# A two-layer hybrid trunk: the instruction threads are merged with other durations, and the merged order is what every engine runs

## The chip, the cores and the metric

The kernel runs on one core of a Trainium2 chip. TensorE (PE) multiplies matrices, VectorE (DVE) and ScalarE (ACT) work on rows of 128 partitions, GpSimd (POOL) adds and multiplies in SBUF, and SyncE (SP) issues the transfers. Each engine takes its instructions one after another, in the order in which they stand in its queue, and waits on semaphores for the others. The metric is the device time of one execution in microseconds, the median of several runs.

## The reference, cut to what matters

The input has 512 tokens of 1024 float32 features. It passes two layers of three sub-layers each: a SwiGLU feed-forward (FFN) at half weight, a mixer, another FFN at half weight. Each sub-layer has a norm before and after:

```python
def swiglu(x, w_in, w_out):
    gate, up = jnp.split(x @ w_in, 2, axis=-1)
    return (jax.nn.silu(gate) * up) @ w_out          # 1024 -> 2 x 2816 -> 1024

def macaron_layer(x, mixer, ...):
    x = x + 0.5 * rmsnorm(swiglu(rmsnorm(x, ffn1_pre_g), ...), ffn1_post_g)
    x = x + rmsnorm(mixer(rmsnorm(x, mix_pre_g)), mix_post_g)
    x = x + 0.5 * rmsnorm(swiglu(rmsnorm(x, ffn2_pre_g), ...), ffn2_post_g)
    return x
```

Layer 0's mixer ("mixer 0") runs RWKV-7 on 8 heads of 64 beside a gated linear recurrence (RG-LRU, 512 features), from one input projection into one output projection. Layer 1's mixer ("mixer 1") is stick-breaking attention with 16 heads of 64: sigmoids of the scores and a running product along the keys.

## The kernel before, in words

Features lie on the partitions, tokens along the row. Every large product is made of three matmuls in the rounded type fp32r: each operand is split into a high and a low part, and high*high, high*low and low*high are added up in a PSUM bank (`mm3`). Most are 128x128 by 128x512; near a sub-layer's border they are 256 wide, since the tokens are there taken in two halves (s0, tokens 0 to 255, and s256), so that one half's norm can run while the other half is still being multiplied.

The work is written as threads, Python generators whose steps each note a few instructions (`Queue`): `weights` splits each weight chunk as it lands (ACT casts the high part, DVE subtracts the low part); `main` issues the large products; `unit_ev`, `third_ev` and `out_ev` empty the banks; `finish` and `add` do the post-norm and the residual of a half, `pre`, `low` and `norm` the splitting of the next normed input and its sum of squares. In mixer 0 each pair of heads passes three threads, `pair`, `inverse` and `chain`, each pair's `pair` waiting for the one before; their matmuls are small plain float32 (64x64 and the like). In mixer 1 the thread `group` makes scores, scans and transposes of one group of queries.

What sets the order: `Run` merges the threads. It keeps a clock per engine, asks `cost` what each instruction takes and when others see its result (`gap`), and always emits the instruction that could start first (`key`, ties by the thread's priority). PE work of `main` has the last priority (9). In the kernel before, `MANUAL` is empty: the merge only numbers the instructions (`cur_priority`, shifted a little by `OFFS`), and the tile framework's scheduler then sorts each engine's queue a second time, by its own view of what is ready and by these numbers. In the profile nearly every instruction carries the line of one call, L366 in `emit`; so groups are told apart by their tiles: `wraw` raw weights, `whi`/`wlo` weight parts, `bank` PSUM, `b` everything in SBUF, `par` parameters.

At each border between sub-layers PE runs two kinds of 256-wide matmul with the tile `ones`: `finish` sums the squares of a half of the output (they are added on POOL, tile by tile), and `norm` those of the next input. What follows one of them in PE's queue stands until POOL's additions are there.

Of the kernel before, what the change touches and what calls it, by code (L numbers as in the profile page):

```python
# [13 lines left out]
F32R = mybir.dt.float32r  # L14
# [5 lines left out]
P = 128  # L20
# [14 lines left out]
MANUAL = ()  # L35
# [17 lines left out]
# ---------------------------------------------------------------- host layout  # L53
# [4 lines left out]
def _consts():  # L58
    """Masks of the shapes alone: for mixer 0 and for mixer 1."""
# [102 lines left out]
# ---------------------------------------------------------------- on the chip  # L162
class Arena:
    """SBUF banks, cut into regions of 64-column units. A bank holds float32 or
    float32r (rounded) regions, and changes its kind when it is empty."""
# [13 lines left out]
    def place(self, k, kind, wide=False):  # L179
        """the region that has been free for the longest, empty banks last"""  # L180
# [82 lines left out]
class Ev:  # L263
    """Something that threads wait for"""
# [5 lines left out]
MEM = object()  # L270

# [10 lines left out]
class Queue:  # L282
    """An engine's instructions, noted for the thread that runs"""
# [9 lines left out]
class Run:  # L293
    """Threads of instructions, merged in the order in which they could start by a
    rough clock of the engines. A thread is a generator; what it notes up to a yield
    may start together, and after all of the step before."""

    TABLES = {AF.Silu: (1,), AF.Sigmoid: (2,), AF.Exp: (3,), AF.Sqrt: (4,), AF.Tanh: (2, 3)}
    SLOW = ("tensor_tensor_scan", "scalar_tensor_tensor")
    FAST = ("tensor_copy", "tensor_scalar", "tensor_scalar_mul", "tensor_scalar_add", "tensor_scalar_max", "memset")  # L300

    def __init__(self, nc):
# [10 lines left out]
        self.hot = False  # L313

# [3 lines left out]
    def warm(self, t, c, cols):  # L318
        """the PE's clock: halved after a tick with few columns"""
# [6 lines left out]

    def cost(self, eng, op, a, k, start):
        """microseconds of an instruction, and until another engine sees its result"""
# [4 lines left out]
        if eng == "pe":  # L333
            w, x = a[1], a[2]
            n, rows = size(x), w.shape[0] / P
            if op == "transpose":
                c, cols = max(w.shape[1], 64) / 1000.0, w.shape[1]
            elif w.dtype == F32R:
                c, cols = max(n, 256) / 2400.0, n * rows
            else:  # L340
                c, cols = n / (750.0 if n <= 64 and min(w.shape) <= 64 else 600.0), 2 * n * rows
            return c * self.warm(start, c, cols), 0.25
        if eng == "dve":
            if op == "reciprocal":
                return 0.07 + 6.3e-3 * n, 0.2
# [1677 lines left out]
```

## Time and profile before

| | |
|---|---|
| three runs | 2137.93, 2146.51, 2146.17 us; median 2146.17 |
| profiled execution | span 2139.7 us from the first to the last instruction; its time with what lies around the span is not listed apart |
| PE | busy 2060.2 us (96%), 11916 records; weight loads 1747.1 us (82%) |
| DVE, ACT, POOL | busy 57%, 40%, 23% |
| granted TensorE clock | mean 0.984 of 2.4 GHz |
| stages | FFN 0 to 362, mixer 0 to 714, two FFNs to 1462, mixer 1 to 1744, FFN to the end |

How to read it: PE's busy time is a union of records that overlap, so short waits between small matmuls do not show as idle time; counts per stretch show more. Idle time of the other engines costs nothing by itself.

### The profile page before, as it was taken

What the parts mean: (1) busy time and instruction counts of PE and PEld (TensorE: products, weight loads), DVE (VectorE), ACT (ScalarE), POOL (GpSimd) and SP (SyncE); (2) the same over time, 40 slices, a digit from 0 to 9 for tenths busy, and PEclk for the clock granted to TensorE, in tenths of its full rate; (3) what the DMA queues carried; (4) which work ended last, traced back from release to release, by engine and by line L of the source; (5) the groups of instructions that cost most, each with busy time, mean ns of one, the idle gap of its engine ahead of it and who ended that gap; (6) DMA issues with size and microseconds to landing.
All of it is one profiled execution on the core that took longest, in us unless ns stands there. A gap on an engine that the chain in (4) does not pass through costs nothing. (4 is left out here: it accounts for less than half of the span.)

```text
span 2139.7 us, 29740 instructions
## 1 busy us (share of the span) xinstructions
PE 2060.2 (96%) x11916; PEld 1747.1 (82%) x11916; DVE 1229.3 (57%) x1770; ACT 863.9 (40%) x1370; POOL 488.5 (23%) x480
## 2 busy tenths in 40 slices
PE   8999999899999899999999999999999899999998
PEld 7888889877677887888898888888878789788887
DVE  6344344887786853444466354446899977344443
ACT  6322223555655443222335322233666755322221
POOL 3000013512331620100153010015232354010013
PEclk9999999999999999999999999999999999999999
DMA  5322321322113223223312322231111223333311
GB/s 195 120 93 99 101 96 51 117 58 62 35 52 104 84 82 116 88 99 108 99 60 81 117 92 98 96 99 36 54 56 60 79 80 108 99 98 99 108 51 40
DMA packets 72378, 185.54 MB, mean 87 GB/s; under 512 B 19632, under 2 KB 26928, under 8 KB 72240
## 3 DMA queue, kind: packets, MB, share of 16 engines
q1 hardware_dynamic: 72240, 183.65, 26.7%
q8 instruction: 93, 1.52, 0.3%
q14 instruction: 45, 0.37, 0.1%
HBM read 177.85 MB, written 5.77 MB: 86 GB/s over the span
## 5 line engine op out<-in xcount | busy, mean ns | idle before, releaser
L366 PE MATMUL bank<-b,b 128*128 128x512 f32 (+6 forms) x7350 | 1232.1, 330 | 28.4 <-DVE b L366 19.5
L366 PEld LDWEIGHTS bank<-b,b 128*128 128x128 f32 (+3 forms) x7350 | 1031.6, 181 | 217.8 <-DVE b L366 36.5
L366 PE MATMUL bank<-b,whi 128*128 128x512 f32 (+1 forms) x2460 | 692.4, 365 | 20.5 <-DVE b L366 10.9
L366 POOL TENSOR_TENSOR b<-b,b 128x256 f32<-128x256 f32 (+5 forms) x355 | 364.3, 1039 | 870.7 <-DVE b L366 560.6
L366 DVE TENSOR_TENSOR b<-bank,b 128x512 f32<-128x512 f32 (+7 forms) x441 | 250.6, 582 | 527.7 <-PE bank L366 520.9
L366 PEld LDWEIGHTS bank<-b,whi 128*128 128x128 f32 x2460 | 441.8, 192 | 92.6 <-DVE b L366 14.3
L366 PE MATMUL bank<-b,wlo 128*128 128x512 f32 (+1 forms) x1230 | 447.7, 364 | 0.8 <-DVE wlo L366 0.8
L366 DVE TENSOR_TENSOR b<-wraw,b 128x1024 fp32r<-128x1024 f32 (+1 forms) x194 | 267.9, 1386 | 148.7 <-ACT b L366 130.4
L366 ACT CAST b<-wraw 128x1024 fp32r<-128x1024 f32 (+1 forms) x194 | 196.6, 1024 | 333.7 <-PE bank L366 192.4
L366 PEld LDWEIGHTS bank<-b,wlo 128*128 128x128 f32 x1230 | 235.9, 192 | 34.9 <-issue 1.2
L366 POOL TENSOR_TENSOR b<-b 128x512 f32<-128x512 f32 (+5 forms) x93 | 105.5, 1144 | 683.2 <-DVE b L366 553.3
L366 ACT ACTIVATE b<-b 128x256 f32<-128x256 f32 (+1 forms) x319 | 154.3, 501 | 243.1 <-DVE b L366 204.9
L366 ACT CAST whi<-wraw 128x1024 fp32r<-128x1024 f32 (+2 forms) x143 | 144.9, 1018 | 238.5 <-PE bank L366 170.8
L366 DVE TENSOR_TENSOR wlo<-wraw,whi 128x1024 fp32r<-128x1024 f32 (+2 forms) x143 | 201.3, 1412 | 68.0 <-ACT whi L366 67.4
L366 ACT CAST b<-b 128x512 fp32r<-128x512 f32 (+3 forms) x188 | 104.8, 560 | 220.1 <-POOL b L366 185.6
L366 DVE TENSOR_TENSOR b<-b,b 128x512 fp32r<-128x512 f32 (+12 forms) x234 | 138.2, 599 | 73.5 <-ACT b L366 72.1
L366 DVE SCALAR_TENSOR_TENSOR b<-b,par,b 128x256 fp32r<-128x256 f32 (+5 forms) x209 | 151.8, 780 | 2.5 <-ACT b L366 2.2
L366 DVE TENSOR_TENSOR_SCAN b<-b,b 128x512 f32<-128x512 f32 (+1 forms) x72 | 71.5, 1019 | 7.2 <-ACT b L366 6.8
L366 ACT COPY b<-bank 128x512 f32<-128x512 f32 (+3 forms) x104 | 50.6, 500 | 61.4 <-PE bank L366 54.9
L366 ACT ACTIVATE b<-b,par 128x256 fp32r<-128x256 f32 (+1 forms) x100 | 51.2, 520 | 54.2 <-POOL b L366 47.5
L366 ACT ACT_TABLE_LOAD x49 | 62.9, 1283 | 9.5 <-PE bank L366 8.0
L366 DVE RECIPROCAL b<-b 128x256 f32<-128x256 f32 (+3 forms) x34 | 42.3, 1243 | 22.0 <-ACT b L366 21.9
(52 smaller groups left out, 623.3 us busy)
## 6 DMA issues: line engine op xcount, KB each, us to landing
wraw<-in_w_dram SPq DMA_DIRECT2D x302, 512.0 KB
wraw<-in_w_dram SPq DMA_DIRECT2D x32, 384.0 KB
b<-in_x_dram SPq DMA_DIRECT2D x16, 128.0 KB
l_mix_residual<-b SPq DMA_DIRECT2D x8, 256.0 KB
b<-l_mix_residual SPq DMA_DIRECT2D x8, 256.0 KB
out_dram<-b SPq DMA_DIRECT2D x16, 128.0 KB
rwkv_scores<-b SPq DMA_DIRECT2D x16, 64.0 KB
b<-in_aux_dram SPq DMA_DIRECT2D x2, 256.0 KB
```

Of the source, the lines that this page charges most:

```text
L366: f(*a, **k)
```

## The change

`MANUAL` names all five engines, so the second sorting is off and each queue holds the merge's own order. `cost` is written anew with other durations by operation, shape and place, with a surcharge where DVE and POOL both work in SBUF; `gap` takes the delay to the next engine from a table by both engines. Transfers keep their cost (bytes by 220 GB/s, 2 us to land). `OFFS` has no effect any more, since nothing sorts by it. `CALLS` gives each thread's instructions a source line of their own and does nothing else; comments are gone. The core of the diff:

```diff
-MANUAL = ()
+MANUAL = ("PE", "DVE", "Activation", "Pool", "SP")
...
+    AFTER = {"dve": {"dve": 0.08, "act": 0.11, "pool": 0.2, "pe": 0.135, "sp": 0.15},
+             "act": {"act": 0.1, "dve": 0.135, "pool": 0.18, "pe": 0.155, "sp": 0.15},
...
+    def matmul(self, op, w, x):
+        n = math.prod(x.shape[1:])
+        if op == "transpose":
+            return 0.109 * max(w.shape[1], 64) / P
+        if w.dtype == F32R:
+            return 0.012 + n / 2380.0
...
-                c, cols = max(n, 256) / 2400.0, n * rows
...
-            return c * self.warm(start, c, cols), 0.25
+            return c * (1.0 if self.warm(start, c, cols) < 2 else 1.6), 0.2
...
-            return (0.12 if op in self.SLOW else 0.07) + (0.55e-3 if op in self.FAST else 1.04e-3) * n, 0.2
+            sb = all(x.space != PSUM for x in [a[0], *aps])
+            c = self.vector(op, n, (len(aps), sb))
+            if sb and n >= 64 and self.clock["pool"] > start:
+                c += min(self.clock["pool"] - start, 1.2 * c)
+            self.shared = start + c if sb else 0.0
+            return c, 0.11
...
-        return 0.1 + (1.1e-3 if op in self.FAST else 2.25e-3) * n, 0.15
+        c = {"memset": 0.08 + 0.8e-3 * n, "tensor_scalar": 0.1 + 1.3e-3 * n}.get(op, 0.17 + 2.1e-3 * n)
+        if self.shared > start:
+            c += min(0.3 * c, self.shared - start)
+        return c, 0.1
...
     def gap(self, th, eng):
-        return th.lat if th.eng != eng else {"dve": 0.09, "act": 0.05, "pool": 0.05}.get(eng, 0.0)
+        return self.AFTER[th.eng].get(eng, th.lat) if th.eng else 0.0
...
-        f(*a, **k)
+        CALLS.get(th.gen.__name__, OTHER)(f, a, k)
```

Three places show what moves. In the changed kernel's rows L280 is `weights`, L283 `pre`, L285 `norm`, L274 `unit_ev`, L276 `third_ev`, L287 `add`, L292 `chain` and L309 `main`.

The first is ACT at the start of the program. `CAST ... <-wraw_74` and `<-wraw_75` are the high parts of the fourth and the fifth weight chunk. Before:

```order
L366 CAST b_19_186<-wraw_74 128x1024
L366 ACTIVATE b_7_101<-b_2_92,par 128x256
L366 ACTIVATE b_8_102<-b_3_93,par 128x256 x2
L366 ACTIVATE b_9_103<-b_4_94,par 128x256 x2
L366 ACTIVATE b_5_95<-b_1_91 128x256
L366 CAST b_21_221<-wraw_75 128x1024
```

And now the stretch from the second of the rows behind the fourth chunk's cast to the fifth chunk's cast:

```order
L285 ACT_TABLE_LOAD
L285 ACTIVATE b_19_186<-bank_86,eps 128x256
L283 ACTIVATE b_6_102<-b_1_91,par 128x256
...
L274 ACT_TABLE_LOAD
L274 ACTIVATE b_19_186<-b_19_186 128x256 x2
L283 ACTIVATE b_9_105<-b_4_94,par 128x256
L285 ACTIVATE b_24_304<-b_2_92 128x256
L283 ACTIVATE b_9_105<-b_4_94,par 128x256
L274 CAST b_20_190<-b_19_186 128x256
L280 CAST b_22_258<-wraw_75 128x1024
```

Six instructions stood between the two casts, eighteen stand there now: eight of `pre`, four squares and the root of `norm`, two table loads, three of `unit_ev`.

The second is POOL at the border between the two FFNs. `b_5_95` is the sum of squares; `b_4_94`, `b_3_93` and other tiles written and read in place are the residual (`add`). Before, the last row is the last square of the output's half s256, and the rows ahead of it, up to the `b_61_2695` row, are seven squares of `norm` with two of `third_ev` between them:

```order
L366 TENSOR_TENSOR b_61_2695<-b_61_2695,b_105_7352 128x256
L366 TENSOR_TENSOR b_5_95<-b_5_95,b_105_7352 128x256
L366 TENSOR_TENSOR b_5_95<-b_5_95,b_109_7913 128x256
L366 TENSOR_TENSOR b_5_95<-b_5_95,b_105_7352 128x256 x2
L366 TENSOR_TENSOR b_5_95<-b_5_95,b_99_6226 128x256
L366 TENSOR_TENSOR b_5_95<-b_5_95,b_105_7352 128x256
L366 TENSOR_TENSOR b_5_95<-b_5_95,b_99_6226 128x256
L366 TENSOR_TENSOR b_5_95<-b_5_95,b_101_6255 128x256
L366 TENSOR_TENSOR b_5_95<-b_5_95,b_107_7853 128x256
L366 TENSOR_TENSOR b_5_95<-b_5_95,b_99_6226 128x256
```

Now the last L276 row is that square:

```order
L285 TENSOR_TENSOR b_5_95<-b_5_95,b_108_7908 128x256
L276 TENSOR_TENSOR b_5_95<-b_5_95,b_99_6227 128x256
L287 TENSOR_TENSOR b_71_4086<-b_71_4086,b_107_7907 128x256
L285 TENSOR_TENSOR b_5_95<-b_5_95,b_107_7907 128x256
L287 TENSOR_TENSOR b_4_94<-b_4_94,b_108_7908 128x256 x2
L276 TENSOR_TENSOR b_5_95<-b_5_95,b_108_7908 128x256
L287 TENSOR_TENSOR b_65_3216<-b_65_3216,b_108_7908 128x256
L285 TENSOR_TENSOR b_5_95<-b_5_95,b_101_6257 128x256
L276 TENSOR_TENSOR b_5_95<-b_5_95,b_101_6257 128x256
L285 TENSOR_TENSOR b_5_95<-b_5_95,b_101_6257 128x256
L285 TENSOR_TENSOR b_5_95<-b_5_95,b_99_6227 128x256 x2
L285 TENSOR_TENSOR b_5_95<-b_5_95,b_107_7907 128x256
```

Three squares of `norm` stand ahead of it, and four behind it.

The third is PE near the end of mixer 0, in the fourth `chain`'s last products (64x64). The 512-wide rows are products of `main` for the output projection. Before:

```order
L366 MATMUL bank_88<-b_59_2652,b_66_3320 64x64
L366 MATMUL bank_90<-b_54_2436,whi_79 128x512
L366 MATMUL bank_88<-b_51_2430,b_3_93 64x64
L366 MATMUL bank_88<-b_59_2652,b_66_3320 64x64
L366 MATMUL bank_90<-b_58_2440,whi_79 128x512
L366 MATMUL bank_88<-b_61_2695,b_3_93 64x64
L366 MATMUL bank_90<-b_54_2436,wlo_80 128x512
L366 MATMUL bank_88<-b_59_2652,b_66_3320 64x64
```

Now:

```order
L292 MATMUL bank_89<-b_28_341,b_70_3519 64x64
L292 MATMUL bank_89<-b_3_93,b_52_2374 64x64
L292 MATMUL bank_89<-b_28_341,b_70_3519 64x64
L292 MATMUL bank_89<-b_3_93,b_52_2374 64x64
L292 MATMUL bank_89<-b_71_4086,b_70_3519 64x64
L292 MATMUL bank_89<-b_3_93,b_52_2374 64x64
L292 MATMUL bank_89<-b_71_4086,b_70_3519 64x64
L309 MATMUL bank_85<-b_77_5020,whi_81 128x512
```

Over the whole of the fourth chain, from its first to its last matmul, PE's queue had some 77 products of `main` in between; it has 13 now.

## Rows read from the trace of the kernel before

**Rows 1.** The page: span, and busy time by engine.
```profile
span 2139.7 us, 29740 instructions
PE 2060.2 (96%) x11916; PEld 1747.1 (82%) x11916; DVE 1229.3 (57%) x1770; ACT 863.9 (40%) x1370; POOL 488.5 (23%) x480
```
**Rows 2.** Busy time by stretch: an FFN, mixer 0, mixer 1, an FFN.
```profile
core 0: us, PE busy (x) PEld busy (x) DVE busy (x) ACT busy (x) POOL busy (x), PEclk, DMA share, GB/s
50.00:350.00 300.00, 299.73 (x1350) 249.03 (x1349) 131.83 (x131) 88.20 (x111) 30.02 (x25) 1.00 0.31 102
420.00:698.00 278.00, 269.72 (x2389) 200.84 (x2387) 203.98 (x476) 153.13 (x236) 68.23 (x60) 0.96 0.23 65
1520.00:1718.00 198.00, 181.78 (x1066) 155.86 (x1065) 184.39 (x306) 133.38 (x261) 62.09 (x63) 0.98 0.20 64
1840.00:2100.00 260.00, 260.00 (x1179) 216.69 (x1179) 103.97 (x104) 69.86 (x86) 23.36 (x19) 1.00 0.26 85
```
**Rows 3.** ACT at the start, in order of time: start, us, operation.
```profile
18.86 2.11 ACT L366 ACTIVATE b<-b,par 128x256 fp32r<-128x256 f32 x5
21.18 1.04 ACT L366 CAST b<-wraw 128x1024 fp32r<-128x1024 f32 x1
22.11 0.72 ACT L366 ACTIVATE b<-b 128x256 f32<-128x256 f32 x2
26.67 1.28 ACT L366 ACT_TABLE_LOAD   x1
27.97 0.47 ACT L366 ACTIVATE b<-bank,eps 128x256 f32<-128x256 f32 x1
30.26 0.42 ACT L366 ACTIVATE b<-b 128x256 f32<-128x256 f32 x1 [0.58 <-DVE b L366]
```
**Rows 4.** PE at the start, in order of time.
```profile
23.36 5.98 PE L366 MATMUL bank<-b,b 128*128 128x256 f32 x47
38.14 0.70 PE L366 MATMUL bank<-b,ones 128*128 128x256 f32 x2 [1.48 <-POOL b L366]
```
**Rows 5.** PE and POOL at the border between the two FFNs, in order of time.
```profile
1107.78 4.23 PE L366 MATMUL bank<-b,b 128*128 128x256 f32 x34
1115.99 1.22 PE L366 MATMUL bank<-b,ones 128*128 128x256 f32 x2 [3.99 <-POOL b L366]
...
1093.45 8.85 POOL L366 TENSOR_TENSOR b<-b,b 128x256 f32<-128x256 f32 x10 [2.08 <-DVE b L366]
1104.55 11.39 POOL L366 TENSOR_TENSOR b<-b,b 128x256 f32<-128x256 f32 x9 [0.58 <-ACT b L366]
```
**Rows 6.** Matmuls of mixer 0 (420 to 698) by shape, count, busy us and mean ns.
```profile
L366 PE MATMUL bank<-b,whi 128*128 128x512 f32 x303 | 109.4, 424 | 1.6 <-DVE b L366 1.6
L366 PE MATMUL bank<-b,wlo 128*128 128x512 f32 x152 | 64.5, 425 | 0.0
L366 PE MATMUL bank<-b,b 128*128 128x512 f32 x51 | 17.0, 422 | 0.4 <-DVE b L366 0.4
L366 PE MATMUL bank<-b,b 64*64 64x64 f32 x928 | 44.0, 230 | 1.0 <-DVE b L366 1.0
```
**Rows 7.** PE in the middle of mixer 0, in order of time.
```profile
538.87 4.44 PE L366 MATMUL bank<-b,b 64*128 64x512 f32 x89
543.25 0.66 PE L366 MATMUL bank<-par,b 128*128 128x128 f32 x4
546.34 1.11 PE L366 MATMUL bank<-par,b 128*128 128x128 f32 x4 [2.44 <-POOL b L366]
```
**Rows 8.** PE at the end of mixer 0, in order of time.
```profile
698.41 1.22 PE L366 MATMUL bank<-b,whi 128*128 128x512 f32 x4 [0.63 <-ACT b L366]
713.60 1.22 PE L366 MATMUL bank<-b,ones 128*128 128x256 f32 x2 [4.21 <-POOL b L366]
```
**Rows 9.** DVE's form of `low` and of the post-norm: ns min/median/max.
```profile
L366 DVE SCALAR_TENSOR_TENSOR b<-b,par,b x209: 379/946/1831, 6.2 to 2121.3; 128x256 fp32r<-128x256 f32 x48, 128x256 f32<-128x256 f32 x44, 128x511 f32<-128x511 f32 x7, 128x510 f32<-128x510 f32 x2
```
**Rows 10.** Busy time and clock around a wait of PE at the border to mixer 0.
```profile
395.00:405.00 10.00, 6.63 (x41) 6.25 (x41) 9.78 (x15) 6.21 (x17) 5.37 (x9) 0.83 0.51 191
405.00:415.00 10.00, 10.00 (x84) 9.95 (x83) 5.61 (x13) 3.13 (x7) 5.62 (x7) 1.00 0.08 28
```

More of the change, by code (lines that the diff above doesn't have):

```diff
@@ L270 @@
 MEM = object()
+CALLS = {
+    "unit": lambda f, a, k: f(*a, **k),
+    "unit_ev": lambda f, a, k: f(*a, **k),
+    "third": lambda f, a, k: f(*a, **k),
+    "third_ev": lambda f, a, k: f(*a, **k),
+    "out_ev": lambda f, a, k: f(*a, **k),
+    "proj": lambda f, a, k: f(*a, **k),
+    "out_sum": lambda f, a, k: f(*a, **k),
+    "weights": lambda f, a, k: f(*a, **k),
+    "loads": lambda f, a, k: f(*a, **k),
+    "presplit": lambda f, a, k: f(*a, **k),
+    "pre": lambda f, a, k: f(*a, **k),
+    "low": lambda f, a, k: f(*a, **k),
+    "norm": lambda f, a, k: f(*a, **k),
+    "post": lambda f, a, k: f(*a, **k),
+    "add": lambda f, a, k: f(*a, **k),
+    "last": lambda f, a, k: f(*a, **k),
+    "one": lambda f, a, k: f(*a, **k),
+    "pair": lambda f, a, k: f(*a, **k),
+    "inverse": lambda f, a, k: f(*a, **k),
+    "chain": lambda f, a, k: f(*a, **k),
+    "rglru": lambda f, a, k: f(*a, **k),
+    "gelu": lambda f, a, k: f(*a, **k),
+    "result": lambda f, a, k: f(*a, **k),
+    "gate": lambda f, a, k: f(*a, **k),
+    "lora": lambda f, a, k: f(*a, **k),
+    "begin": lambda f, a, k: f(*a, **k),
+    "scores": lambda f, a, k: f(*a, **k),
+    "head": lambda f, a, k: f(*a, **k),
+    "attend": lambda f, a, k: f(*a, **k),
+    "group": lambda f, a, k: f(*a, **k),
+    "unit_v": lambda f, a, k: f(*a, **k),
+    "v_ev": lambda f, a, k: f(*a, **k),
+    "out": lambda f, a, k: f(*a, **k),
+    "home": lambda f, a, k: f(*a, **k),
+    "stash": lambda f, a, k: f(*a, **k),
+    "unstash": lambda f, a, k: f(*a, **k),
+    "main": lambda f, a, k: f(*a, **k),
+    "finish": lambda f, a, k: f(*a, **k),
+}
+OTHER = lambda f, a, k: f(*a, **k)
 class Thread:
@@ L313, in __init__ @@
         self.hot = False
+        self.shared = 0.0
     TICK = 3.413
@@ L325, in warm, with vector @@
         return 1.0 if self.hot else 2.0
+    def matmul(self, op, w, x):
[4 more added lines that the diff above has]
+            return 0.012 + n / 2380.0
+        rows, cols = w.shape[0], math.prod(w.shape[1:])
+        if n <= 2:
+            return 0.112
+        if rows <= 64 and cols <= 64:
+            return 0.045 * n / 64
+        if n <= 64:
+            return 0.054 if cols <= 64 else 0.08
+        return 0.02 + 4 * n / 2380.0 * (0.5 if cols <= 64 or rows <= 64 else 1.0)
+    def vector(self, op, n, ins):
+        full, sb = ins
+        if op == "reciprocal":
+            return 0.06 + 6.3e-3 * n
+        if op == "tensor_tensor_scan":
+            return 0.06 + 2.1e-3 * n
+        if full == 1 and sb and op != "tensor_reduce":
+            return 0.06 + 0.65e-3 * n
+        return 0.065 + 1.04e-3 * n
     def cost(self, eng, op, a, k, start):
```

22 lines of the change are left out of this document (10 added, 12 removed).

## The prediction

> **What bounds the kernel now.** I read the page's busy line first [rows 1]: of 2139.7 us PE is busy 2060.2, so all idle time that PE shows is 79.5 us, 3.7% of the span; DVE has 57%, ACT 40%, POOL 23%. Then the busy times by stretch [rows 2]. In an FFN (50 to 350 us) PE is busy 299.73 of 300 us, DVE 132, ACT 88, POOL 30: nothing but PE counts there, and 1350 matmuls at .222 us each stay whatever their order. The change moves instructions and neither adds nor removes arithmetic, so about 1,400 of the 2140 us, the FFNs, can't change inside. What can change is the start, the borders between stages, and the two mixers, where the small steps of `chain`, `unit`, `third` and `inverse` pass from engine to engine. In mixer 1 (1520 to 1718) DVE, at 184.39 of 198 us, is fuller than PE at 181.78 [rows 2].
>
> The median of the three runs, 2146.17, is 6.5 us above the profiled span. I work out a new span and add 6.5.
>
> **The start.** PE's first long row begins at 23.36 [rows 4], when the fifth weight chunk's high part has been cast: ACT's cast row for that chunk starts at 21.18 and takes 1.04, so it ends at 22.22; the five `pre` activations ahead of it took 2.11, .42 each [rows 3]. In the new order eighteen instructions stand between the fourth chunk's cast and the fifth's, where six stood. Priced by the rows of the same operations: eight `pre` 8 × .42 = 3.4; four squares 4 × .36 = 1.4 (.72 for two); two table loads 2 × 1.28 = 2.6; the root .47; two activations of `unit_ev` at .42, .8; one 256-wide cast, taken as one activation, .4. That is 9.1 us. The stretch begins behind the fourth chunk's cast, which before was over about 18.0, just ahead of the five `pre`; 18.0 + 9.1 + 1.04 = 28.1, against 23.36 when PE now begins with that chunk. So PE waits some 5 us. What could hide it is PE's work on the first four chunks, which is used up by then; were all of it spread by other products that now stand earlier, the cost is 0, and with waits of ACT for POOL and DVE among these eighteen it is 8. I take +5, range 0 to +8. Why the merge does this: it still prices a transfer at bytes by 220 GB/s plus 2 us, so the clock at which it believes the chunk arrives is not this trace's.
>
> **The borders.** Between the two FFNs PE stops 3.99 us for POOL [rows 5]. The last square of the output's half s256 is on POOL, behind seven squares of `norm`; ten such operations take 8.85 us, .885 each. Now three squares stand ahead of it: 4 × .885 = 3.5 us earlier at best. But four `add`s, all of which `norm` of s0 needs, now stand among them, and on PE the ones-matmul that waits for the s256 sum comes 28 products earlier than before: rows 5 give 34 such products 4.23 us, .124 each, so 3.5 us of cover is gone from ahead of the wait. Gain and loss cancel. The next product in the queue is `norm`'s, whose four `add`s (4 × .885 = 3.5 us) are late next. At the border to mixer 0 the same pattern gave a wait of about three microseconds and then a stretch at granted clock .83 on average [rows 10], that is, part of it at 1.2 instead of 2.4 GHz; a border wait costs itself and up to about as much again. I see one wait shortened and others lengthened there (the ones-matmuls of `norm` stand earlier on PE too; at 38.14 one already waits 1.48 us for POOL [rows 4]). Four borders, each ±2.5: 0, range −10 to +10.
>
> **Mixer 0** (420 to 698). PE shows only 278 − 269.72 = 8.3 us idle [rows 2], which would be the least that waits hold. But the records of small matmuls overlap, so I also count. 303 + 152 + 51 = 506 products are 512 wide [rows 6]; at .222, as in the FFN, they are 112 us. The other 2389 − 506 = 1883 records, at .050 (89 of the 64-wide triangle's in 4.44 us [rows 7]), are 94 us. Sum 206, so waits hold at most 278 − 206 = 72 us. A third reading lies between: weight loads are busy 200.84 of 278, 72%, against 249.03 of 300, 83%, in the FFN; at the FFN's density the same loads would take 200.84 / .83 = 242 us, so 36 us are waits. Where those come from can be seen singly: at 543.9 PE stops 2.44 us for POOL before four small products [rows 7] whose operand is a transposed tile of the first chain, and eight ready products of `inverse` stood behind them; the new order has eleven other instructions in between. An order made with durations near the trace's can fill such waits because DVE (73%), ACT (55%) and POOL (25%) have room. Between 8.3 and 72 I go by the nearest stretch, the 36, and take 6 off for the end of the mixer, which comes apart below: −30, range 0 to −72.
>
> The page "Perfetto Trace Analysis" of the Trainium skill, section "Identifying the Most-Contended Engine", says that busy matmul time is a poor measure since matmuls are pipelined, and that weight-load time is a good one. By the busy share alone (97%) the mixer could give back 8.3 us and the sum would be about zero; by the weight loads' (72%), 36. The counts of rows 6 agree with the page.
>
> **The end of mixer 0.** Over the fourth chain some 77 products of `main` stood between its matmuls and 13 do now. 64 × .222 = 14.2 us of cover is moved behind or ahead of it. If the chain runs at the pace of its latencies, the mixer gets longer by all of that; if the products fill what was empty before, by nothing. Behind the mixer PE stopped 4.21 us for POOL, until 713.60 [rows 8], and the products moved back can stand there: 14.2 − 4.2 = 10. I take +10, range 0 to +14.2.
>
> **Mixer 1.** DVE is idle 198 − 184.39 = 13.6 us and PE 16.2 [rows 2]. With DVE at 93% no order gains more than about 13; I take half, −7, and since DVE could also be delayed by POOL (62 us busy beside it), the range is +5 to −13.
>
> The remaining edits are priced at nothing: `CALLS` only labels lines; `OFFS` only served the second sort; SP's queue holds no work that PE waits for behind the start, DMA engines being 20 to 31% busy by stretch [rows 2]; at the start they are in the term above.
>
> **Sum.** +5 + 0 − 30 + 10 − 7 = −22. Span 2139.7 − 22 = 2117.7, and with 6.5 the time is 2124.
>
> **Rivals.**
>
> B, no change: the waits are not misfits of the order but latencies from engine to engine, and durations that no table of constants can give. For it: DVE's one form of `low` and the post-norm takes 379 to 1831 ns, median 946 [rows 9], for much the same tiles; a fixed queue order made with one price is wrong by up to a microsecond at each step, whichever price. And a sort that had placed instructions by its own times of arrival is taken away. Against it: waits such as that at 543.9 are plain misplacements. Then the mixers give back some 5 us, which the start takes: 2146.
>
> The page "SBUF — State Buffer" of the Trainium skill, section "Who interferes with whom", says that DVE and GpSimd hold their shared SBUF ports exclusively, for a whole instruction, so that the second one blocks until the first is done. The new cost is a smooth surcharge, at most 1.2 of DVE's duration; under a lock, who waits is decided by which comes first, and an order computed ahead of time would miss it. The spread of rows 9, 379 to 1831, agrees with the page more than with a surcharge; by that rule the mixer term would be near 0.
>
> C, slower: the fourth chain of mixer 0 loses its fill. With 13 products instead of 77 beside it PE runs on the chain's latencies from about 660 us, the 14.2 us of products follow later as work in addition, and the sparse stretch risks the lower clock as in rows 10. With the start's 5, and mixers that give nothing back, 2146 + 14.2 + 5 = 2165. It decides as soon as what the rest of both mixers gives back is less than about 8 us: 19 − 8 = 11, half a per cent over. For it: PE is bound by work almost everywhere, so cover given away early is missing later. Against it: products used earlier in the mixer are used where PE waited, so they are not lost.
>
> That the change does not do what it says is in part already so: transfers aren't priced from the trace, which is the start's term.
>
> **How the numbers follow.** Half a per cent, about what a measurement of this kernel can tell, is 10.7 us: 2135.4 to 2156.9 is the same. My forecast, 2124, with its own range of 2100 to 2140, has .55, of which .05 lies within the half per cent; B .22, near 2146; C .23, around 2165. Faster .50, same .27, slower .23. The bounds of all terms together (−95 to +37) are wider than I believe at once, since mixer 0 can't give back every latency; below I stop at 2096 (mixer 0 at −58), above at 2166, just past C's price.
>
> **What would show it.** Start: the fifth chunk's cast ends near 28, and PE has a wait of 5 us there. Border between the FFNs: POOL's wait stays 3 to 5 us. Mixer 0: its length falls from 278 towards 250 with the weight loads' share rising from 72% towards 80%, and the 2.44 us wait at 543.9 is gone; in its fourth chain waits for DVE and ACT show on PE, and the 4.21 at its end is gone. Mixer 1: DVE above 95%. I am wrong if the weight loads' share in mixer 0 stays at 72% (B), or if the stretch from the fourth chain's start to the next FFN's first product is longer by more than 14 us (C).

## The result and the profile after

The changed kernel takes 2152.41 us, median of ten runs (2148.02 to 2158.26); the kernel before, in the ten runs beside them, 2141.75 (2137.67 to 2146.51). The ratio is 1.0054, with a 95% interval of 1.0039 to 1.0069: slower by about 11 us, where 22 us less were forecast.

First the page of the changed kernel, span and busy time, which answers to [rows 1]:

```profile
span 2150.2 us, 29766 instructions
PE 2048.2 (95%) x11916; PEld 1751.8 (81%) x11916; DVE 1211.3 (56%) x1770; ACT 858.1 (40%) x1369; POOL 501.9 (23%) x480
```

The work is the same, the span 10.5 us longer. Where, the busy times by stretch tell (columns as in [rows 2]; mixer 0 and mixer 1 lie a little later now):

```profile
50.00:350.00 300.00, 299.73 (x1343) 248.41 (x1342) 128.76 (x132) 87.57 (x111) 32.71 (x21) 1.00 0.32 104
427.00:725.00 298.00, 270.55 (x2566) 218.41 (x2565) 226.52 (x505) 164.34 (x257) 80.76 (x79) 0.94 0.25 73
1532.00:1728.00 196.00, 182.54 (x1060) 158.10 (x1059) 179.40 (x300) 133.93 (x258) 62.57 (x64) 0.97 0.22 70
1840.00:2100.00 260.00, 259.20 (x1143) 214.08 (x1142) 106.75 (x107) 73.34 (x90) 28.06 (x17) 1.00 0.29 92
```

And mixer 0 of the kernel before, between the same two products of `main`:

```profile
415.00:724.00 309.00, 296.10 (x2566) 225.53 (x2565) 228.44 (x509) 168.62 (x260) 83.94 (x74) 0.96 0.23 67
```

The FFNs stand still, as [rows 2] let expect. Mixer 0 is 11 us shorter, with the same 2566 matmuls. So some 22 us must have been lost elsewhere. To find them I counted the products of `main` in PE's order, which is the same list in every kernel, and took the times at which certain ones begin. A stretch "FFN to mixer 0" runs from the last product of the FFN to the 235th of the mixer (behind a mixer or between FFNs to the 469th; into mixer 1 to the 290th). The rest of each FFN differs by at most 0.4 us between any two kernels. The first row of the table is the kernel before in us; all others are differences to it. It holds all experiments, since most of them are read from it. Each row comes from one execution; ten executions of the kernel before lie up to 9 us apart (2137.67 to 2146.51), so a few microseconds in one cell can be what a single kernel does by itself.

| kernel | start | FFN to mixer 0 | mixer 0 | to FFN | FFN to FFN | FFN to mixer 1 | mixer 1 | to FFN | five borders |
|---|---|---|---|---|---|---|---|---|---|
| before | 42.1 | 37.4 | 308.9 | 91.8 | 85.3 | 46.7 | 230.1 | 85.5 | 346.7 |
| changed | +6.7 | +5.0 | -11.6 | -4.1 | +7.0 | +4.6 | -2.7 | +5.9 | +18.5 |
| new_costs_sorted | -1.2 | +1.4 | +18.9 | -1.1 | +4.6 | +5.4 | +1.9 | +2.3 | +12.7 |
| old_costs_unsorted | +7.0 | +12.3 | -2.0 | +0.4 | +8.8 | +8.5 | +1.7 | +10.0 | +40.0 |
| sorted_no_offsets | +3.8 | +7.9 | -24.9 | +2.3 | +4.6 | +3.4 | 0.0 | +6.9 | +25.1 |
| new_sorted_no_offsets | +4.0 | +9.3 | -19.8 | -3.5 | +5.3 | +1.6 | +4.9 | +7.4 | +20.2 |
| no_chain_offset | -0.4 | -1.1 | -17.5 | +0.2 | 0.0 | 0.0 | +0.1 | +0.6 | -0.3 |
| start_faster_loads | +3.4 | +9.1 | -9.0 | -4.0 | +2.9 | +3.6 | -0.4 | +7.4 | +19.0 |
| norm_after_low | +6.6 | +3.6 | -10.0 | -1.0 | +4.9 | -0.5 | -2.8 | +4.7 | +11.7 |
| norm_in_turn | +7.2 | +3.5 | -3.7 | -4.7 | +4.1 | +1.4 | -3.8 | +8.7 | +12.9 |
| norm_in_turn_start | +1.0 | +0.4 | -6.0 | -5.3 | +4.4 | +1.5 | -3.7 | +8.7 | +9.6 |
| norm_both_in_turn | +1.5 | -0.3 | -2.1 | -6.5 | +1.4 | -0.9 | -1.2 | +5.2 | -1.0 |
| nudge_delay | +6.1 | +6.1 | -0.7 | -4.4 | +3.1 | +4.7 | -4.4 | +5.9 | +15.4 |
| nudge_delay_2 | +7.1 | +4.9 | -11.6 | -3.5 | +4.8 | +3.8 | +1.3 | +6.5 | +16.6 |
| nudge_before | -0.6 | +1.0 | +9.8 | -3.9 | -0.7 | +3.8 | +9.7 | +3.8 | +4.0 |
| nudge_before_2 | -0.8 | -0.4 | +26.2 | -3.9 | +0.7 | +2.9 | +4.1 | +5.6 | +4.8 |

The changed kernel loses 6.7 us at the start and 18.5 at the borders, and its mixers give back 14.3.

**The start.** ACT of the changed kernel, answering to [rows 3]; the first row is the fourth chunk's cast, the last the fifth's:

```profile
16.43 1.03 ACT L280 CAST b<-wraw 128x1024 fp32r<-128x1024 f32 x1
...
17.89 1.28 ACT L285 ACT_TABLE_LOAD   x1
...
23.58 1.28 ACT L274 ACT_TABLE_LOAD   x1
...
26.90 1.04 ACT L280 CAST b<-wraw 128x1024 fp32r<-128x1024 f32 x1
```

PE, answering to [rows 4]:

```profile
21.18 3.04 PE L309 MATMUL bank<-b,b 128*128 128x256 f32 x24
27.99 0.80 PE L309 MATMUL bank<-b,b 128*128 128x256 f32 x2 [3.78 <-ACT b L280]
30.59 5.15 PE L309 MATMUL bank<-b,b 128*128 128x256 f32 x29 [1.80 <-DVE b L280]
```

The cast ended at 27.94 where 28.1 had been worked out, and PE waited for it (3.78), and then for the low part of the same chunk (1.80). From 28 to 32 us the granted clock was .50.

**A border.** DVE of the changed kernel between the two FFNs. L310 is `finish` (root and post-norm of the second half), L274 `unit_ev` of the first half:

```profile
1113.44 1.75 DVE L285 RECIPROCAL b<-b 128x256 f32<-128x256 f32 x1
1115.11 0.39 DVE L310 SCALAR_TENSOR_TENSOR b<-b,par,b 128x256 f32<-128x256 f32 x1
1115.41 0.42 DVE L274 TENSOR_TENSOR b<-bank,b 128x256 f32<-128x256 f32 x1
1116.21 0.42 DVE L274 TENSOR_TENSOR b<-bank,b 128x256 f32<-128x256 f32 x1 [0.38 <-PE bank L309]
1119.08 0.42 DVE L274 TENSOR_TENSOR b<-bank,b 128x256 f32<-128x256 f32 x1 [2.44 <-PE bank L309]
1119.42 3.52 DVE L310 SCALAR_TENSOR_TENSOR b<-b,par,b 128x256 f32<-128x256 f32 x5
```

Behind the first of eight post-norm operations stand three `unit_ev` of the other half, and the third waits 2.44 us for a product; seven post-norms stand behind it, which need nothing that the first one did not have. POOL, which adds what they give (L287), answers with a wait:

```profile
1115.58 0.73 POOL L287 TENSOR_TENSOR b<-b,b 128x256 f32<-128x256 f32 x1 [3.96 <-DVE b L310]
1119.97 0.91 POOL L287 TENSOR_TENSOR b<-b,b 128x256 f32<-128x256 f32 x1 [3.66 <-DVE b L310]
1120.85 0.92 POOL L274 TENSOR_TENSOR b<-b 128x256 f32<-128x256 f32 x1
1121.73 1.80 POOL L287 TENSOR_TENSOR b<-b,b 128x256 f32<-128x256 f32 x2
1123.50 0.92 POOL L274 TENSOR_TENSOR b<-b,b 128x256 f32<-128x256 f32 x1
...
1130.53 0.91 POOL L287 TENSOR_TENSOR b<-b,b 128x256 f32<-128x256 f32 x1
```

In the kernel before the same eight adds are one row:

```profile
1120.11 7.09 POOL L366 TENSOR_TENSOR b<-b,b 128x256 f32<-128x256 f32 x8 [4.17 <-DVE b L366]
```

7.09 us there, 15.9 (1115.58 to 1131.44) in the changed kernel. The first half's eight adds, which lie ahead of these rows, are stretched too, by squares of `third_ev` (L276) and of `norm` (L285) among them. Their first and their last:

```profile
1090.08 0.91 POOL L287 TENSOR_TENSOR b<-b,b 128x256 f32<-128x256 f32 x1 [2.26 <-DVE b L310]
...
1103.09 0.91 POOL L287 TENSOR_TENSOR b<-b,b 128x256 f32<-128x256 f32 x1
```

That is 13.9 us; the kernel before has the same eight, with two squares between them, in the 8.85 us of [rows 5]. PE waits for `low` (L284) of either half, which comes behind that half's adds. Its rows, answering to [rows 5]; the first three wait for the first half's `low`, the last three for the second half's:

```profile
1102.59 0.62 PE L309 MATMUL bank<-b,b 128*128 128x256 f32 x3 [0.92 <-DVE b L284]
1103.46 0.62 PE L309 MATMUL bank<-b,b 128*128 128x256 f32 x3 [0.25 <-DVE b L284]
1106.00 4.25 PE L309 MATMUL bank<-b,b 128*128 128x256 f32 x16 [1.92 <-DVE b L284]
...
1130.90 0.62 PE L309 MATMUL bank<-b,b 128*128 128x256 f32 x3 [0.26 <-DVE b L284]
1131.77 0.62 PE L309 MATMUL bank<-b,b 128*128 128x256 f32 x3 [0.25 <-DVE b L284]
1133.51 6.18 PE L309 MATMUL bank<-b,b 128*128 128x256 f32 x39 [1.12 <-DVE b L284]
```

None of these waits is as long as the single 3.99 us of [rows 5], and their sum is not much more (4.7 us in the rows shown). What differs is the clock. Busy times in 5 us of the changed kernel:

```profile
1106.00:1111.00 5.00, 5.00 (x18) 4.07 (x18) 5.00 (x4) 2.91 (x6) 4.76 (x5) 0.50 0.46 142
1111.00:1116.00 5.00, 4.43 (x19) 4.15 (x19) 4.18 (x5) 2.37 (x4) 1.04 (x2) 0.51 0.49 173
...
1131.00:1136.00 5.00, 3.63 (x17) 3.22 (x18) 3.00 (x5) 2.04 (x4) 2.06 (x3) 0.69 0.00 0
```

and of the kernel before, its only stretch below 1.00 there:

```profile
1115.00:1120.00 5.00, 4.00 (x19) 3.83 (x20) 2.56 (x4) 0.47 (x1) 0.94 (x1) 0.66 0.47 156
```

PE shows 5.00 of 5.00 us busy and does 18 matmuls where the full clock does 42 ([rows 10]: 84 in ten). It was fed operand by operand, and the granted clock was 1.2 GHz for ten microseconds, then low once more. An estimate of what the clock took, from PE's busy time in these stretches: 5.00 × .50 + 4.43 × .49 + 3.63 × .31 = 5.8 us, against 4.00 × .34 = 1.4 before, so 4.4 of the 7.0 us that this border lost. By halves: after 48 of the border's products the changed kernel is 9.2 us behind; the kernel before loses 6.2 of this in its own wait of 3.99 us and the slow stretch after it (2.9 are left at the 144th product); the second half's waits add 5.1 by the 216th.

At the border to mixer 1 the second half alone does it. `unit_ev` and what follows it stand on DVE ahead of six of the second half's eight `low`, and PE waits, first in the changed kernel, then in the kernel before:

```profile
1505.84 0.58 PE L309 MATMUL bank<-b,whi 128*128 128x256 f32 x1 [7.61 <-DVE b L284]
1494.34 0.39 PE L366 MATMUL bank<-b,whi 128*128 128x256 f32 x1 [3.03 <-DVE b L366]
```

### The profile page after: what moved, and what is told of

It reads as the page before. It is cut to its first block, busy times and chain, and to the rows that moved or that the text cites. A ratio compares the mean times of both kernels' runs of the same rounds, so it can differ in the third digit from the quotient of the medians.

```text
span 2150.2 us, 29766 instructions
## 1 busy us (share of the span) xinstructions
PE 2048.2 (95%) x11916; PEld 1751.8 (81%) x11916; DVE 1211.3 (56%) x1770; ACT 858.1 (40%) x1369; POOL 501.9 (23%) x480
## 5 line engine op out<-in xcount | busy, mean ns | idle before, releaser
L309 PE MATMUL bank<-b,b 128*128 128x512 f32 (+1 forms) x5379 | 1060.3, 355 | 31.8 <-DVE b L284 25.0
L309 PEld LDWEIGHTS bank<-b,b 128*128 128x128 f32 x5379 | 896.7, 192 | 176.5 <-DVE b L284 32.5
L309 PE MATMUL bank<-b,whi 128*128 128x512 f32 (+1 forms) x2488 | 700.6, 366 | 22.7 <-DVE b L284 9.8
L309 PEld LDWEIGHTS bank<-b,whi 128*128 128x128 f32 x2488 | 451.8, 193 | 96.1 <-DVE b L284 11.6
L309 PE MATMUL bank<-b,wlo 128*128 128x512 f32 (+1 forms) x1244 | 452.7, 364 | 0.5 <-DVE b L291 0.5
L274 DVE TENSOR_TENSOR b<-bank,b 128x512 f32<-128x512 f32 (+1 forms) x237 | 145.3, 619 | 403.4 <-PE bank L309 402.7
L280 DVE TENSOR_TENSOR b<-wraw,b 128x1024 fp32r<-128x1024 f32 (+1 forms) x192 | 255.3, 1330 | 94.0 <-ACT b L280 93.9
L280 ACT CAST b<-wraw 128x1024 fp32r<-128x1024 f32 (+1 forms) x192 | 195.6, 1023 | 211.3 <-PE bank L309 153.6
L309 PEld LDWEIGHTS bank<-b,wlo 128*128 128x128 f32 x1244 | 240.9, 194 | 34.6 <-DVE wlo L280 1.4
L280 ACT CAST whi<-wraw 128x1024 fp32r<-128x1024 f32 (+2 forms) x145 | 147.2, 1017 | 252.5 <-PE bank L309 170.6
L280 DVE TENSOR_TENSOR wlo<-wraw,whi 128x1024 fp32r<-128x1024 f32 (+2 forms) x145 | 198.8, 1372 | 52.6 <-ACT whi L280 52.5
L274 POOL TENSOR_TENSOR b<-b 128x512 f32<-128x512 f32 (+1 forms) x50 | 71.7, 1437 | 571.9 <-DVE b L274 538.0
L274 ACT CAST b<-b 128x512 fp32r<-128x512 f32 (+3 forms) x160 | 88.7, 555 | 278.3 <-POOL b L274 269.1
L274 POOL TENSOR_TENSOR b<-b,b 128x512 f32<-128x512 f32 (+1 forms) x50 | 74.7, 1496 | 503.1 <-DVE b L274 464.9
L276 DVE TENSOR_TENSOR b<-bank,b 128x256 f32<-128x256 f32 (+1 forms) x88 | 47.9, 544 | 191.8 <-PE bank L309 191.6
L274 DVE TENSOR_TENSOR b<-b,b 128x512 fp32r<-128x512 f32 (+3 forms) x140 | 90.1, 646 | 74.2 <-ACT b L274 73.4
L274 ACT ACTIVATE b<-b 128x512 f32<-128x512 f32 (+1 forms) x100 | 57.3, 577 | 107.8 <-DVE b L274 107.8
L287 POOL TENSOR_TENSOR b<-b,b 128x256 f32<-128x256 f32 x87 | 81.2, 944 | 25.9 <-DVE b L310 25.9
L285 POOL TENSOR_TENSOR b<-b,b 128x256 f32<-128x256 f32 x84 | 78.3, 932 | 35.7 <-ACT b L285 34.3
L284 DVE SCALAR_TENSOR_TENSOR b<-b,par,b 128x256 fp32r<-128x256 f32 x96 | 70.5, 766 | 2.3 <-ACT b L283 2.2
L276 POOL TENSOR_TENSOR b<-b,b 128x256 f32<-128x256 f32 (+1 forms) x51 | 43.7, 856 | 98.1 <-ACT b L276 98.1
```

The source lines that it names most:

```text
L274: "unit_ev": lambda f, a, k: f(*a, **k),
L276: "third_ev": lambda f, a, k: f(*a, **k),
L280: "weights": lambda f, a, k: f(*a, **k),
L284: "low": lambda f, a, k: f(*a, **k),
L285: "norm": lambda f, a, k: f(*a, **k),
L287: "add": lambda f, a, k: f(*a, **k),
```

## The experiments

**The two halves of the change apart.** The change has two parts, the second sorting off and the new durations, and four combinations.

new_costs_sorted, the changed kernel with

```diff
-MANUAL = ("PE", "DVE", "Activation", "Pool", "SP")
+MANUAL = ()
```

> The changed kernel with the second sorting switched on again (MANUAL empty), so only the new durations differ from the kernel before. Theory 1 (the lost second sorting makes the start and the borders longer, the new durations make the mixers shorter): the start and four borders come back to the kernel before's lengths, mixers stay 12 and 6 us shorter, so about 2125 to 2132 us, a ratio of 0.991 to 0.996 to the kernel before. Theory 2 (the new durations themselves order the borders badly): still about 2150, ratio 1.003 to 1.006. Theory 3 (the sorting undoes what the merge does, whatever its durations): 2142, ratio 0.998 to 1.002.

2172.01 us, ratio 1.0152 (1.0134 to 1.0169). The start comes back (-1.2), the borders only from 18.5 to 12.7, and mixer 0 is 18.9 us longer. Between the FFNs DVE has the kernel before's order again (below), and the loss has another place: the ones-matmul of [rows 5] waits 8.41 us instead of 3.99, since a square of `third_ev` stands on POOL behind those of `norm`:

```profile
1134.47 1.22 PE L310 MATMUL bank<-b,ones 128*128 128x256 f32 x2 [8.41 <-POOL b L276]
```

old_costs_unsorted, the kernel before with the reverse of that line.

> The kernel before with the second sorting off on all five engines and its old durations kept: the other half of the change. Theory 1: start and borders get longer by 20 to 30 us and nothing is given back in the mixers, so 2162 to 2185 us, ratio 1.010 to 1.020. Theory 2: within 0.3% of the kernel before, 2142 us. Theory 3: the same as theory 1, since a merge by rough durations needs the sorting.

2187.71 us, ratio 1.0220 (1.0204 to 1.0236). By the ratios the sorting off alone costs 47 us, the durations alone 33, both together 12: they are not to be added. Without sorting the new durations give 35 us back (2188 to 2152), 21 of them at the borders; under the sorting they cost 33, 19 of them in mixer 0. No theory had the first run right; theory 1 comes near in the second and has the place of the loss: start and borders lose 25 us in the one kernel without sorting and 47 in the other, where it named 20 to 30. Theory 2 has a part: with the new durations the borders lose 12.7 us even under the sorting.

**What the sorting did at the borders.** It held `norm`, `weights` and `unit_ev` back by 100, 50 and 50 places (`OFFS`). DVE's order between the two FFNs, with L and l for the `low` of the first and second half, N for the root of the first half, u for its `unit_ev` out of the banks; what else stands between them is left out:

```
before               L L L L L L L L l l l l l l l l N u u u u u u
changed              L L L L L L L L N u u u u u l l l u l l l l l
sorted_no_offsets    L L L L L L L L N u u u u u l l l u l l l l l
new_costs_sorted     L L L L L L L L l l l l l l l l N u u u u u u
```

sorted_no_offsets, the kernel before with

```diff
-OFFS = {"norm": -100, "weights": -50, "unit_ev": -50, "chain": -20}
+OFFS = {}
```

> The kernel before with an empty table OFFS: the second sorting stays, but norm, weights, unit_ev and chain are no longer held back in it by 100, 50, 50 and 20 places. If the holding back of norm and unit_ev at the borders is what the changed kernel lost: the borders get longer by 10 to 25 us, 2152 to 2167 us, ratio 1.005 to 1.012. If it is the sorting by times of arrival as such: within 0.2% of the kernel before.

2146.31 us, ratio 1.0028 (1.0016 to 1.0039). The borders lose 25.1 us and the start 3.8, with the old durations and the sorting: so much the holding back was worth there, and the changed kernel has lost it. With the new durations it is worth less: the borders lose 12.7 us with it (new_costs_sorted) and 20.2 without it (new_sorted_no_offsets, below). So the changed kernel's 18.5 us are not all the lost table; the new durations order the borders worse by themselves. What was not expected is that mixer 0 gets 24.9 us shorter, and so the time is below the 2152 to 2167 us expected. `chain` was the likeliest entry for that.

no_chain_offset, the same with only `"chain": -20` taken out.

> The kernel before with chain taken from OFFS (norm, weights and unit_ev stay held back in the second sorting). With an empty OFFS the borders cost 29 us more and mixer 0 gave 25 back. If the holding back of chain by 20 places is what costs mixer 0 those 25 us: borders as in the kernel before, mixer 0 about 284 us instead of 309, 2113 to 2122 us, ratio 0.987 to 0.993. If mixer 0 gained from the other entries of OFFS: within 0.3% of the kernel before, 2134 to 2146 us.

2124.69 us, ratio 0.9929 (0.9909 to 0.9948): the borders as before (-0.3), mixer 0 shorter by 17.5. This is the fastest kernel of the study, faster than both, if 3 us above the expected range: mixer 0 is 291 us long and not 284. Holding `chain` back costs mixer 0 some 20 us: with it and the sorting mixer 0 was 309, 319, 328 and 335 us long in four kernels, without it 284, 289 and 291.

new_sorted_no_offsets, the changed kernel with the sorting on and `OFFS` empty.

> The changed kernel with the second sorting on and OFFS empty. With OFFS the new durations under the sorting gave 2172 us, with 19 us lost in mixer 0 against the kernel before and the borders nearly as before. If what costs mixer 0 there is the holding back of chain, unit_ev and weights: mixer 0 gives back 25 to 45 us, the borders lose 20 to 30, 2145 to 2175 us, and mixer 0 is 270 to 285 us long. If the sorting's own times of arrival spoil the order in mixer 0: it stays at 320 us or more, and the time is 2190 to 2200.

2151.04 us, ratio 1.0048 (1.0032 to 1.0064). Mixer 0 falls from 327.7 to 289.1: the sorting does not spoil the new durations there, the holding back did. That it was `chain`'s is shown with the old durations alone.

**The start.** start_faster_loads, the changed kernel with

```diff
-            return max(0.5, a[0].shape[0] * size(a[0]) * 4 / 220e3), 2.0
+            return max(0.5, a[0].shape[0] * size(a[0]) * 4 / (350e3 if start < 40 else 220e3)), 2.0
```

> The changed kernel, with transfers that the merge places before 40 us of its clock priced at 350 GB/s (the trace shows 330 to 380 in full slices) instead of 220; all else as in the changed kernel. If the start's loss of 7 us comes from the place of the fifth chunk's cast behind eighteen instructions: the cast ends 3 to 5 us earlier, the wait of 3.8 and 1.8 us on PE at 24 us is gone, and the time is 2145 to 2149, ratio to the kernel before 1.002 to 1.004. If another wait takes its place: 2152, ratio 1.005.

2155.84 us, ratio 1.0076 (1.0061 to 1.0091). The start got 3.3 us shorter as expected (the fifth chunk's cast at 22.94 instead of 26.90, one wait of 1.48 left), but the border behind it 4.1 us longer and mixer 0 2.6: one price at the start moves ties in the whole program. The total was a miss, the start a hit.

**The borders mended in the merge.** norm_after_low, the changed kernel with one line of `norm`:

```diff
-            yield Ev(self.run.new.t + LAG[2])
+            yield Ev(self.run.new.t + LAG[2]) if sub.first else self.h_ev[sub, HALVES[1].start, KT - 1]
```

> The changed kernel with one line of norm altered: from the second sub-layer on, the root of the first half (its ones-matmuls, reciprocal and so the unit_ev behind it) waits in the merge for the last low of the second half, which is the order that the kernel before has at all five borders and the changed kernel at none. If the borders' 18 us in the changed kernel come from that (the adds, pre and low of the second half stand among unit_ev and norm of the first): DVE's stretch from the reciprocal of finish to the last low falls from 20 to about 11 us, each border gets 3 to 6 us shorter, 2130 to 2140 us, ratio to the kernel before 0.996 to 1.001. If it is the durations and delays in general: 2148 to 2156, ratio 1.004 to 1.008.

2145.79 us, ratio 1.0017 (1.0004 to 1.0031). That lies between the two ranges expected. DVE's order is as before, the borders lose 11.7 instead of 18.5. Between the FFNs the rest is a wait that the edit itself made; PE there:

```profile
1127.18 0.59 PE L285 MATMUL bank<-b,ones 128*128 128x256 f32 x2
1132.02 1.22 PE L285 MATMUL bank<-b,ones 128*128 128x256 f32 x2 [4.25 <-POOL b L285]
```

The second half's ones-matmul stood right behind the first half's, and its squares still among the adds on POOL.

norm_in_turn keeps this wait for the first half's root alone and puts the squares of the second half behind its last add:

```diff
+            if s.start and not sub.first:
+                yield self.x_ev[sub, s.start, KT - 1]
             for k in range(KT):
...
-            yield Ev(self.run.new.t + LAG[2])
+            yield Ev(self.run.new.t + LAG[2]) if sub.first or s.start else self.h_ev[sub, HALVES[1].start, KT - 1]
```

> The changed kernel with two lines in norm, from the second sub-layer on: the first half's root waits for the last low of the second half (as in norm_after_low), and the second half's squares wait for the second half's last add. In norm_after_low the squares still stood between POOL's adds (10.8 to 12.4 us for eight instead of 7.1), and the second half's ones-matmul stood right behind the first half's on PE, which waited 4.25 us there. If interruption of the second half's chain is what the borders lose: eight adds take 7.1 us again, the wait of 4.25 is gone, the five borders come within 5 us of the kernel before's in sum, 2128 to 2138 us, ratio 0.994 to 0.999. If not: the borders still lose 12 us or more, 2142 to 2152.

2158.15 us, ratio 1.0085 (1.0070 to 1.0099): a miss. The eight adds took 7.1 us again, but the wait did not go, it moved to the same ones-matmul at its new place:

```profile
1140.28 1.16 PE L285 MATMUL bank<-b,ones 128*128 128x256 f32 x2 [4.21 <-POOL b L285]
```

The borders lost 12.9, so an uninterrupted chain alone isn't it: what stands behind the wait in PE's queue counts too.

norm_in_turn_start adds the price of start_faster_loads, and the same order of halves in the first sub-layer.

> norm_in_turn, with the root of the first sub-layer's first half behind the second half's last low too, and transfers before 40 us priced at 350 GB/s in the merge. If the start's 6.5 us are the fifth chunk's cast and the same interruption: product 234 of the first FFN is issued at 42 to 44 us instead of 48.8, and the time is 4 to 7 us below norm_in_turn. If the start is bound by something else: 47 us or later, no difference.

2143.71 us, ratio 1.0016 (1.0006 to 1.0026). The start is at +1.0 instead of +7.2: there the price and the order together were the cause. The time fell by 14 us where 4 to 7 were expected; 6 of them are the start.

norm_both_in_turn takes the two waits that were left: the squares of the first half behind its last add too, and 4 us in `LAG[2]` for the second half's ones-matmul.

```diff
-            if s.start and not sub.first:
+            if not sub.first:
                 yield self.x_ev[sub, s.start, KT - 1]
...
+            yield Ev(self.run.new.t + (0.0 if sub.first or not s.start else LAG[2]))
```

> norm_in_turn_start, with two more edits from the second sub-layer on: the first half's squares wait for the first half's last add as well (they stood among the adds on POOL, and low of the first half ended 4 us later than in the kernel before), and the second half's ones-matmul is placed as if its sum of squares came 4 us later (PE waited 4.5 us at it between the FFNs, with products ready behind it). If these two waits, with the half clock behind each, are what the borders still lose: the border between the two FFNs and that to the last FFN fall to at most 2 us above the kernel before's, all four borders to -8 to +2 in sum, and the time is 2126 to 2138 us, ratio 0.993 to 0.999, mixer 0 anywhere between 297 and 308. If other waits take their place: 2140 to 2150.

2135.28 us, ratio 0.9981 (0.9970 to 0.9993). Time, mixer 0 and the sum of the borders (-1.0) are within what was expected. POOL's adds of the second half between the FFNs:

```profile
1112.70 7.08 POOL L287 TENSOR_TENSOR b<-b,b 128x256 f32<-128x256 f32 x8 [1.34 <-DVE b L310]
```

So what the changed kernel lost at start and borders, 25 us, is undone by three rules in `norm`, a delay and one price, with its durations and without the sorting. The sum is even, but not each border: that behind mixer 0 is 6.5 us shorter than in the kernel before, and that to the last FFN stays at +5.2 where at most 2 were expected. Nor did the first half's part go: between the FFNs this kernel is 7.2 us behind after 48 products, since PE still waits for the first half's `low` there. And mixer 0, at -2.1, gives less than in the changed kernel.

**How far the order alone moves the time.** nudge_delay changes one delay in `AFTER`:

```diff
-             "pe": {"pe": 0.0, "dve": 0.2, "act": 0.2, "pool": 0.25, "sp": 0.25},
+             "pe": {"pe": 0.0, "dve": 0.21, "act": 0.2, "pool": 0.25, "sp": 0.25},
```

> The changed kernel with the delay from PE to DVE in the table AFTER at 0.21 instead of 0.20 us, which says nothing new about the chip. It measures how far the time moves when the merge takes other decisions at near ties. If the 10.7 us of the change are a matter of such luck: the time moves by 8 us or more either way. If they are a matter of the order's rules: within 5 us of 2152, and the borders stay longer than before's by 15 to 25 us together.

2158.00 us, ratio 1.0082 (1.0062 to 1.0101). nudge_delay_2 does the same with "act".

> The changed kernel with the delay from PE to ACT in AFTER at 0.21 instead of 0.20 us. The first nudge moved mixer 0 by +11 us and the borders with the start by less than 4 in sum. If mixer 0's length under the merge alone is a matter of near ties: it comes out anywhere between 285 and 310 us (measured from product 234 to product 935), while start and borders lose 18 to 27 us against the kernel before once more. If the first nudge hit one place: mixer 0 at 297 again, 2149 to 2155 us.

2154.40 us, ratio 1.0070 (1.0056 to 1.0084). Mixer 0 is at -0.7 in the one and at -11.6 in the other; start and borders lose 21.5 and 23.7, against 25.2 in the changed kernel. So the loss stays in all three draws, and eleven microseconds in mixer 0 are within what ties decide.

nudge_before has 1.05 for 1.04 ns in the kernel before's price of a DVE column, nudge_before_2 has 1.03.

```diff
-            return (0.12 if op in self.SLOW else 0.07) + (0.55e-3 if op in self.FAST else 1.04e-3) * n, 0.2
+            return (0.12 if op in self.SLOW else 0.07) + (0.55e-3 if op in self.FAST else 1.05e-3) * n, 0.2
```

> The kernel before with one price of DVE at 1.05 instead of 1.04 ns for a column, second sorting on. If the order of the mixers is as sensitive there: mixer 0 moves by 5 us or more from 309, and the borders stay within 5 us in sum since the sorting holds norm back. If the kernel before is a chosen optimum of this search, the time is longer, by 3 to 20 us; if the sorting smooths it, within 4 us of 2141.

> The kernel before with the same price of DVE at 1.03 instead of 1.04 ns for a column (1.05 made it 22 us slower, 20 of them in the mixers). If the kernel before is a picked draw among orders that differ by ties: slower again, 2146 to 2170 us, the most of it in the mixers, the borders within 5 us in sum. If 1.05 hit one bad place: 2138 to 2144 us.

2162.16 us (ratio 1.0101, 1.0083 to 1.0118) and 2174.78 us (1.0165, 1.0146 to 1.0185). Both are a little slower than was expected of a draw that had been picked. The borders move by 5 us, the mixers by 20 and 30. Mixer 0 of the second:

```profile
414.00:749.00 335.00, 311.78 (x2567) 235.66 (x2566) 230.64 (x489) 167.32 (x259) 86.64 (x76) 0.91 0.21 62
```

and the shortest of the study, sorted_no_offsets:

```profile
427.00:711.00 284.00, 269.47 (x2562) 210.70 (x2561) 221.35 (x499) 168.96 (x259) 84.80 (x74) 0.99 0.26 73
```

The same matmuls at clock .91 and .99. The kernel before is the best of three draws for its prices: one per cent more or less on one of them costs 22 or 35 us. The changed kernel was compared with that draw.

## Why the prediction was wrong

Forecast were 22 us less, the table has some 11 more. Of the 33 between them the borders make 18.5, mixer 0 with its end 8.4, mixer 1 4.3 and the start 1.7. The 6.5 us that the prediction added from span to time show in no run: the changed kernel's profiled execution took 2151.94 us at a span of 2150.2, 1.7 more.

- **The start** was right in mechanism and within its bounds: 5 worked out, 0 to 8, measured 6.7; the cast's end came out within 0.2 us. PE waited 3.78 for it; the low part's wait, 1.80, and the half clock behind both were not in the sum.
- **The borders** are the step that failed: "Gain and loss cancel", 0 with bounds of ±10, measured +18.5 (and five borders, where four were counted). Priced were waits of PE for POOL at the ones-matmuls. What PE waits for there in the changed kernel is mostly `low`, from DVE, one operand after another. The kernel before has such waits too: the one beside [rows 10], which the prediction took for "the same pattern" as POOL's, is

```profile
399.18 0.58 PE L366 MATMUL bank<-b,b 128*128 128x256 f32 x1 [3.37 <-DVE b L366]
```

  Not priced was that squares would stand among the first half's adds on POOL (8.9 us became 13.9), and `unit_ev` of the first half in DVE's queue among the second half's post-norms, waiting there for a product (eight adds went from 7.1 to 15.9 us). Removing `OFFS` was read as without effect, "only served the second sort", without asking what the sort did by it; sorted_no_offsets shows 25 us for just that with the old durations, and some 7 with the new ones. And the price of waits was taken as their length and about as much again, while several waits below 2 us were followed by ten microseconds at 1.2 GHz.
- **Mixer 0 and its end**: -20 in the sum, -11.6 measured. The sign held here, but the nudges, with -0.7 and -11.6, say that a gain of this size can't be put down to better durations. The reading by weight loads, 36 us of waits, is more than any order here gave back (24.9 at most). Their share was forecast to rise from 72% towards 80% and is 218.41 / 298 = 73%, as in the kernel before (225.53 / 309 = 73%); by the prediction's own sign that speaks for B. The page "Perfetto Trace Analysis" of the Trainium skill, section "Identifying the Most-Contended Engine", takes weight-load time for the better measure. In this case its share hardly told orders 51 us apart: 74, 73, 73 and 70% in mixers 0 of 284, 298, 309 and 335 us. The loads themselves took 210.70 us at a mean clock of .99 and 235.66 at .91. The busy share did worse, as the page has it: 95, 91, 96 and 93%.
- **The end of mixer 0**, +10 in the sum, rival C's mechanism: its waits did show. In the fourth chain PE waits for DVE between steps of four small products:

```profile
671.85 0.33 PE L292 MATMUL bank<-b 64*64 64x64 f32 x4 [2.26 <-DVE b L292]
672.57 0.48 PE L292 MATMUL bank<-b 64*64 64x64 f32 x4 [0.39 <-DVE b L292]
...
675.17 0.48 PE L292 MATMUL bank<-b 64*64 64x64 f32 x4 [0.39 <-DVE b L292]
```

  The 4.21 us of [rows 8] are gone as forecast, and so is the 2.44 of [rows 7]. But the stretch that was to show C, from the fourth chain's start to the next FFN's first product, is not longer: 58.5 us before (665.8 to 724.3), 57.9 now (666.8 to 724.7). So the term was -0.6 and not +10, and the -11 us lie ahead of the fourth chain, where -30 had been forecast. C named the right sign by the wrong place: the loss came from the start and the borders.
- **Mixer 1**: -7 in the sum, -2.7 measured, within the bounds; DVE did not rise above 95% but is at 179.40 of 196, 92%.
- **Rival B** had part of it: taking the sorting away costs, by 47 us with the old durations. But it was named for its times of arrival; what these runs show of it is its table of places. That B's 2146 us lie nearest to the measured time is chance: it had 5 us back from the mixers, and they gave 14.3. Its spread of [rows 9] mixes tiles, too: the 128x256 operations lie between 379 and 1022 ns, the 1831 is a 509-wide one.

What stays open: why the sorting with the new durations loses in mixer 0 exactly where it holds `chain` back (only the sum is shown), why the new durations order the borders worse, and the 5.2 us at the border to the last FFN; they arise in its first 24 products, where PE waits for the first half's `low`. Whether DVE and POOL hold each other up by the rule that the prediction weighed was not tested.

## What to carry to other kernels

When a pass that orders instructions is taken away, ask what each of its tables did at the places where stages meet, and read that from the order of one queue there: which half's instructions stand in front of which, and what they wait for. Compare a schedule with a handful of its neighbours (one price moved by a per cent) before a gain or loss of one per cent is put down to a reason; what shows in all of them can have a reason, the rest may be the draw. A border's price is its waits and the stretch at half clock behind them; between the FFNs here, feeding PE operand by operand cost more of it than one wait of about the same length.

## What had not been expected of the hardware

Feeding a queue in small steps was paid in clock: between the FFNs waits of 0.92, 0.25 and 1.92 us were followed by ten microseconds at 1.2 GHz (granted .50 and .51), and one wait of 3.99 us by a stretch of .66 over five. POOL's add of 128x256 took 0.73 us at 1115.58, where DVE read a bank, and 0.90 to 0.92 in the rows from 1119.97 to 1131.44, beside DVE's work in SBUF; single ones took up to 1.7 (1097.11). That DVE is the cause was not tested.
